# Seven-product input projection: third weight sum in DRAM, one addition in place, new order of products

## The chip, the cores and the metric

The kernel runs on one core of one Trainium2 chip. The metric is the device time of one execution in microseconds (us); a shorter time is better. A profiled execution is recorded by the hardware profiler, and its trace gives the start and end of each instruction on each engine: PE (TensorE, with PEld for its weight loads), DVE (VectorE), ACT (ScalarE), POOL (GpSimd), SP (SyncE, which here only issues transfers). Names with a q behind them (SPq, ACTq, POOLq) are the engines' instruction queues.

## The reference

One decoder layer over 512 tokens of width 2048, in float32. A normed input is projected to 8 heads of forgetting attention ("fox") and 8 heads of a three-branch attention ("nsa"); both are joined, projected back and added to the input; then follows a gated feed-forward network.

```python
def reference(x, attn_norm, w_in, ..., w_gate, w_up, w_down):
    h = _rms_norm(x, attn_norm[l])
    x = x + _hybrid_mixer(h, w_in[l], ...)       # proj = h @ w_in; fox and nsa heads; @ w_out
    h = _rms_norm(x, ffn_norm[l])
    x = x + _swiglu(h, w_gate[l], w_up[l], w_down[l])

# fox head: softmax over past keys of q.k * scale + cum_f[query] - cum_f[key], times v
# with q and k normed per head and cum_f the running sum of log-sigmoid forget gates
```

## The kernel before

Each product is made in full precision from float32 parts: an operand x is split into a high part (ScalarE copies it to the format float32r, line 95) and a low part (VectorE subtracts, line 92), and TensorE sums high times high, high times low and low times high.

The program has four stages. In the first (to about 460 us in the trace) plain projections of 24 tiles of `w_in` run among the heads of nsa. In the second (460 to 730 us) the other 16 tiles, the queries, keys and values of the fox heads 2 to 7, are projected in eight pairs of tiles (`PAIRS`), among the fox heads themselves. The third projects back with `w_out`; the fourth is the feed-forward network (from 908 us). The change concerns the second stage and what prepares it.

A pair isn't projected by eight block products (two halves of the tokens, two tiles, two halves of the depth) but by seven, in the manner of Strassen (`seven`, lines 1049 to 1093). The operands from the activations are `form(f, u)`: f = 0 to 3 lie in `bigm`, f = 4 to 6 are made beforehand by `forms_45` and `forms_6`, and the upper half of `bigm` is made ready for f = 3 by `forms_3`. With the pair's weight blocks b1 = `win[i, 0]`, b2 = `win[i + 1, 0]`, b3 = `win[i, 1]` and b4 = `win[i + 1, 1]` the weight operands are

| product f | weights | from where |
|---|---|---|
| 0 | b1 | loaded |
| 5 | b1 + b2 + b4 | first sum in DRAM (`fsum` 0) |
| 1 | b3 | loaded |
| 4 | b1 + b2 | b2 added in place to the tile of f = 0 |
| 2 | b1 + b2 + b3 + b4 | second sum in DRAM (`fsum` 1) |
| 6 | b4 | loaded |
| 3 | b2 + b4 | b4 loaded, b2 added in place |

That is also their order; in the last pair f = 3 comes before f = 6. A product is 24 matmuls of 128 x 256 (line 1071).

Weights come through three staging tiles of 128 x 1024 float32 (`ws0` to `ws2`, `ws_tile`). `fetch` loads one from SP's queue (line 98) as soon as the parts of its last content are split; `split_w` writes the parts into one of two tiles `wp`, so that ScalarE and VectorE can work one product ahead of TensorE. An addition in place (`add12`, line 1047) is two accumulating transfers of 256 KB on GpSimd's queue, issued after the tile's load has landed and, for f = 4, after the tile has been split for f = 0.

The sums in DRAM are made by transfers from DRAM to DRAM on GpSimd's queue (`sum_weights`, line 141), each of 256 KB, copying or accumulating. `in_weight_sums` makes those of the pairs (20 pieces for two pairs, `GROUP`), `out_weight_sums` those of the projection back (`osum`, 48 pieces). `split_w` issues `paced[0]` of them for each weight split and lets each wait for a split two before it. GpSimd also makes the biases of the scores (`nb`, line 816, and `nbf`, line 845), in the same queue.

Every engine runs its instructions in the order in which the program was put down. `weave`, `gated` and `among` interleave the steps of projections, heads and forms by counts; `stagger` lets the end of a pair (norms of its keys and queries, or transposes of its values) run among the products of the next. `ahead_of` runs generators of forms one behind the other and starts the next one's loads (`xf`, line 968, on ACT's queue) a given number of generators ahead.

## Time and profile before

| | |
|---|---|
| time, median of 3 runs | 2174.6 us (2172.25 to 2176.71) |
| profiled execution | 2173.53 us, of which its span is 2171.5 us |
| mean granted clock of TensorE | 0.982 |
| PE busy | 2092.0 us (96%) |
| DVE busy | 1776.7 us (82%) |
| ACT busy | 1074.8 us (49%) |
| POOL busy | 352.7 us (16%) |
| transfers | 424.78 MB, mean 196 GB/s |

Busy times are sums over the span from the first to the last instruction. In the rows of the trace a transfer or instruction stands as output<-input by the program's names; [4.77 <-ACT wp_kf L95] behind a row says that the engine stood idle 4.77 us before it, until that instruction had ended. A view of waits lists who waited for whom: total us, times, longest.

### The profile page before, as it was taken

The page shows a single profiled execution, that of the slowest core. Times are in us where ns is not written, and L with a number is a line of the kernel's source. Part 1 is how long each engine was busy: PE and PEld are TensorE (multiplying, and loading weights), DVE is VectorE, ACT ScalarE, POOL GpSimd, SP SyncE. Part 2 cuts the span into 40 slices and gives each one's busy share as a digit, 9 for nine tenths or more (in the row PEclk, how much of TensorE's full clock was granted, in tenths as well). Part 3 has the DMA queues.
Part 4 walks back from the last instruction along what each step waited for, and adds up shares of the span by engine and source line. Part 5 has one row for each costly group of instructions (what it writes and reads, how often), then busy time and mean ns, then how long its engine had stood idle before and what let it go on. Part 6 is the DMA issues. An engine that isn't in the chain of part 4 may idle for free.

```text
span 2171.5 us, 40270 instructions
## 1 busy us (share of the span) xinstructions
PE 2092.0 (96%) x16219; PEld 2002.8 (92%) x16219; DVE 1776.7 (82%) x2725; ACT 1074.8 (49%) x1433; POOL 352.7 (16%) x528
## 2 busy tenths in 40 slices
PE   9999999877788899999999999999999999999999
PEld 8888988777787799899999999999999999999999
DVE  6777677655655687899999999999999997879898
ACT  6556465544545555544443434444344455556554
POOL 1133232222332101111111111111111100000000
PEclk9999999988998999999999999999999999999999
DMA  6656455667887557567766777777777798569865
GB/s 217 199 141 133 134 143 140 165 171 183 195 214 165 184 182 239 181 182 193 195 192 179 208 184 202 187 195 191 181 204 185 197 350 291 151 212 328 311 170 153
DMA packets 145644, 424.78 MB, mean 196 GB/s; under 512 B 17768, under 2 KB 17768, under 8 KB 145456
## 3 DMA queue, kind: packets, MB, share of 16 engines
q1 hardware_dynamic: 90016, 285.01, 39.1%
q0 software_dynamic: 43920, 102.00, 25.1%
q10 hardware_dynamic: 11520, 35.18, 4.5%
q8 instruction: 127, 2.08, 0.4%
q14 instruction: 61, 0.50, 0.1%
HBM read 389.86 MB, written 111.95 MB: 231 GB/s over the span
## 4 chain that ended last, share of the span: by engine, by line
PE 79%; DMA 6%; DVE 5%; issue 5%; ACT 4%; POOL 1%; ACTq 0%; SPq 0%; DVEq 0%; POOLq 0%
PE q L1779 39%; PE pd L1918 13%; PE pd L1923 6%; DMA ws_pair<-win 4%; PE po L1363 2%; PE ps_vs L535 2%; DMA xf<-xT 2%; PE ps_kf L1071 1%; PE ps_qn L256 1%; PE ps_qn L257 1%; PE ps_qn L258 1%; PE po L258 1%; PE po L257 1%; PE po L256 1%; ACT wp_kf L95 1%
## 5 line engine op out<-in xcount | busy, mean ns | idle before, releaser
L95 ACT ACTIVATE bigm<-r 128x1792 fp32r<-128x1792 f32 x174 | 298.2, 1714 | 454.2 <-PE q L1779 272.6
L92 DVE TENSOR_TENSOR bigm<-r,bigm 128x1792 fp32r<-128x1792 f32 x174 | 351.4, 2020 | 11.3 <-ACT bigm L95 10.6
L92 DVE TENSOR_TENSOR r<-r 128x512 f32<-128x512 f32 x522 | 267.0, 512 | 27.5 <-DMA r<-wgu 15.1
L141 POOL DMA_DIRECT2D wsum<-wdn x176 | 120.1, 689 | 701.6 <-ACT bigm L95 602.7
L1779 PE MATMUL q<-bigm 128*128 128x256 f32 x1848 | 217.0, 276 | 0.0
L1779 PE MATMUL q<-formy,bigm 128*128 128x256 f32 x1848 | 216.8, 276 | 0.0
L1779 PE MATMUL q<-forma,bigm 128*128 128x256 f32 x1848 | 216.8, 276 | 0.0
L1779 PE MATMUL q<-formx,bigm 128*128 128x256 f32 x1848 | 216.8, 276 | 0.0
L1779 PEld LDWEIGHTS q<-bigm 128*128 128x128 f32 x1848 | 213.1, 188 | 0.0
L1779 PEld LDWEIGHTS q<-forma,bigm 128*128 128x128 f32 x1848 | 213.0, 188 | 0.1
L1779 PEld LDWEIGHTS q<-formy,bigm 128*128 128x128 f32 x1848 | 212.9, 188 | 0.1
L1779 PEld LDWEIGHTS q<-formx,bigm 128*128 128x128 f32 x1848 | 212.9, 188 | 0.0
L1918 PE MATMUL pd<-bigm 128*128 128x256 f32 x1200 | 146.9, 276 | 0.0
L1918 PEld LDWEIGHTS pd<-bigm 128*128 128x128 f32 x1200 | 141.0, 188 | 0.0
L92 DVE TENSOR_TENSOR bigm<-wd,bigm 128x1024 fp32r<-128x1024 f32 (+1 forms) x62 | 107.7, 1738 | 12.5 <-ACT bigm L95 12.4
L95 ACT ACTIVATE bigm<-rawm 128x768 fp32r<-128x768 f32 (+2 forms) x72 | 66.0, 926 | 98.4 <-PE pd L1923 64.1
L1071 PE MATMUL ps_kf<-bigm,wp_kf 128*128 128x256 f32 x576 | 84.2, 305 | 26.7 <-ACT wp_kf L95 26.7
L1071 PEld LDWEIGHTS ps_kf<-bigm,wp_kf 128*128 128x128 f32 x576 | 79.5, 214 | 28.7 <-ACT wp_kf L95 28.7
L92 DVE TENSOR_TENSOR wp_kf<-ws_pair,wp_kf 128x1024 fp32r<-128x1024 f32 x42 | 51.3, 1222 | 55.5 <-ACT wp_kf L95 55.0
L95 ACT ACTIVATE bigm<-wd 128x1024 fp32r<-128x1024 f32 (+1 forms) x62 | 91.1, 1469 | 9.4 <-DVE wd L92 6.1
L92 DVE TENSOR_TENSOR bigm<-rawm,bigm 128x768 fp32r<-128x768 f32 (+2 forms) x72 | 75.5, 1058 | 23.5 <-ACT bigm L95 22.8
L1923 PE MATMUL pd<-bigm 128*128 128x256 f32 x600 | 80.7, 276 | 0.0
(630 smaller groups left out, 4381.1 us busy)
## 6 DMA issues: line engine op xcount, KB each, us to landing
r<-wgu SPq DMA_DIRECT2D x174, 512.0 KB, 4.4
wsum<-wdn POOLq DMA_DIRECT2D x176, 256.0 KB, 5.1
rawm<-ad SPq DMA_DIRECT2D x44, 512.0 KB, 6.7
wd<-wdn SPq DMA_DIRECT2D x40, 512.0 KB, 6.1
wd<-wsum SPq DMA_DIRECT2D x40, 512.0 KB, 7.1
ad<-cb ACTq DMA_DIRECT2D x22, 896.0 KB, 6.5
rawm<-ad SPq DMA_DIRECT2D x44, 384.0 KB, 3.6
ws_pair<-win SPq DMA_DIRECT2D x32, 512.0 KB, 5.0
```

The source lines that it names most:

```text
L92: return pin(nc.vector.tensor_tensor(*args, op=op))
L95: return pin(nc.scalar.activation(*args, **kw))
L141: d = nc.gpsimd.dma_start(step[0], step[1], **step[2])
L256: nc.tensor.matmul(o, lh, rh, start=start, stop=False)
L257: nc.tensor.matmul(o, lh, rl, start=False, stop=False)
L258: nc.tensor.matmul(o, ll, rh, start=False, stop=stop)
L535: nc.tensor.matmul(z[2 * b + t][:, :cols[n]], x[:, xp, at], wp[n][kk], start=(c == 0 and kk == 0 and n == 0 and (t == 0 or gcols is not No ...
L1071: nc.tensor.matmul(z, w[wp][:, u * P:(u + 1) * P], form(f, u)[xp], start=(fresh and m == 0), stop=(m == len(todo) - 1), skip_group_check=True)
L1363: nc.tensor.matmul(q[b][:, h * 256:(h + 1) * 256], w[wp][:, u * P:(u + 1) * P], a[xp], start=(h == 0 and u == 0 and wp == 0 and xp == 0), ...
L1779: nc.tensor.matmul(o, w[wp][:, fb, cs], a[:, xp, fa], start=(k == 0 and h == 0 and wp == 0 and xp == 0), stop=(g == NG - 1 and kk == 1 and ...
L1918: nc.tensor.matmul(b[q][k][:, h * 256:(h + 1) * 256], w[0][:, fb, q * P:(q + 1) * P], a[xp][:, fa], start=(j == 0 and h == 0 and xp == 0), ...
L1923: nc.tensor.matmul(b[q][k][:, h * 256:(h + 1) * 256], w[1][:, fb, q * P:(q + 1) * P], a[0][:, fa], start=False, stop=(j == NJ - 1), skip_g ...
```

## The change

Each pair gets a third sum in DRAM, b2 + b4 (`fsum` 2), which f = 3 loads as it is; the second addition in place is gone. `GROUP` becomes 28. From the second pair on the order is 0, 5, 1, 3, 4, 2, 6: f = 3 goes on in the PSUM bank of f = 5, and three products lie between f = 0 and f = 4 where two did; the first pair keeps 0, 5, 1, 4, 2, 6, 3. `fetch` now takes the next load of one list (`wanted`) into whatever tile has just been split, and first makes sure that the pair's sums have been issued. The number of sums for each split goes from 2, 2.4, 1 and 0.95 to 3, 3, 2 and 0.75 in the four parts of the first two stages. The forms are loaded two generators ahead instead of one, and the first two of `forms_3` start before the stage. In the last pair the saved heads are fetched four steps earlier, and four instead of two heads are split there.

```diff
--- before.py
+++ after.py
@@ -159,9 +159,9 @@
                     yield s[t][:, i], s[t0][:, i], {"accum_op": OP.add}
 
     PAIRS = [("p", h) for h in (2, 3, 4)] + [("v", 4)] + [("p", h) for h in (5, 6, 7)] + [("v", 6)]
-    fsum = {p: [dr.tile([P, 2, T], F32, name=f"fsum{p[0]}{p[1]}{t}") for t in range(2)] for p in PAIRS}
+    fsum = {p: [dr.tile([P, 2, T], F32, name=f"fsum{p[0]}{p[1]}{t}") for t in range(3)] for p in PAIRS}
     FIRST7 = PLAIN
-    GROUP = 20
+    GROUP = 28
     emitted = [0]
 
     def in_weight_sums():
@@ -173,14 +173,14 @@
         for n0 in range(0, len(PAIRS), 2):
             two = [(fsum[PAIRS[n]], blocks(n)) for n in (n0, n0 + 1)]
             cols = [slice(i * T, (i + 1) * T) for i in range(2)]
-            for t, k in ((0, 0), (1, 2)):
+            for t, k in ((0, 0), (1, 2), (2, 3)):
                 for s, b in two:
                     for i in range(2):
                         yield s[t][:, i], b[k][:, cols[i]], {}
-            for k in (1, 3):
+            for t, k in ((0, 1), (2, 1), (0, 3)):
                 for s, b in two:
                     for i in range(2):
-                        yield s[0][:, i], b[k][:, cols[i]], {"accum_op": OP.add}
+                        yield s[t][:, i], b[k][:, cols[i]], {"accum_op": OP.add}
             for s, b in two:
                 for i in range(2):
                     yield s[1][:, i], s[0][:, i], {"accum_op": OP.add}
@@ -931,7 +931,7 @@
         yield
 
     N, NS, F, FS = 18, 25, 53, 13
-    paced[0] = 2
+    paced[0] = 3
     tokens_out = unload()
     weave(ks0, itertools.islice(tokens_out, 2), N, 2, 11)
     weave(stagger(values(("vs0", "vw0"), gcols), normed("kw0", gain(V_WK), "kv"), nsa_q(0), nsa_q(1)),
@@ -1028,23 +1028,35 @@
         return [S[f, u][:, xp] for xp in range(2)]
 
     fetched = {}
-    WS = {0: 0, 5: 1, 1: 2, 2: 1}
-
-    def fetch(n, f):
-        if n == len(PAIRS):
+
+    def products(n):
+        if n == 0:
+            return (0, 0), (1, 5), (0, 1), (2, 4), (1, 2), (2, 6), (0, 3)
+        return (0, 0), (1, 5), (0, 1), (1, 3), (2, 4), (1, 2), (2, 6)
+
+    wanted = iter([(n, f) for n in range(len(PAIRS)) for _, f in products(n) if f != 4])
+
+    def fetch(at):
+        key = next(wanted, None)
+        if key is None:
+            ws_turn.append(at)
             return
+        n, f = key
+        while emitted[0] < GROUP * (n // 2 + 1):
+            sum_weights(highs[-1], osums)
+            emitted[0] += 1
         i = FIRST7 + 2 * n
-        src = {0: win[i, 0], 5: fsum[PAIRS[n]][0], 1: win[i, 1], 2: fsum[PAIRS[n]][1]}.get(f, win[i + 1, 1])
-        if f in (5, 2):
-            src = src.rearrange("p i c -> p (i c)")
-        fetched[n, f] = ws_tile(f"pair{n}_{f}", ws_turn[0] + n + WS.get(f, 2 * ((f == 6) ^ (n == len(PAIRS) - 1))))
-        load(fetched[n, f], src)
-
-    def add12(n, f):
+        src = {0: win[i, 0], 1: win[i, 1], 6: win[i + 1, 1]}.get(f)
+        if src is None:
+            src = fsum[PAIRS[n]][{5: 0, 2: 1, 3: 2}[f]].rearrange("p i c -> p (i c)")
+        fetched[key] = ws_tile(f"pair{n}_{f}", at), at
+        load(fetched[key][0], src)
+
+    def add12(n):
 
         for c in range(2):
             c = slice(c * T, (c + 1) * T)
-            nc.gpsimd.dma_start(fetched[n, f][:, c], win[FIRST7 + 2 * n + 1, 0][:, c], accum_op=OP.add)
+            nc.gpsimd.dma_start(fetched[n, 0][0][:, c], win[FIRST7 + 2 * n + 1, 0][:, c], accum_op=OP.add)
 
     def seven(key, names):
 
@@ -1052,13 +1064,12 @@
         t0, t1 = [ftile(f"t_{name}") for name in names]
         b = []
         lower, upper = slice(0, 256), slice(256, 512)
-        last = [(2, 6), (0, 3)][::-1 if n == len(PAIRS) - 1 else 1]
-        for step, (to, f) in enumerate([(0, 0), (1, 5), (0, 1), (2, 4), (1, 2)] + last):
-            w = split_w(fetched[n, f if f != 4 else 0], HALF * P, f"{names[0]}_{step}", 3)
-            nn, ff = ((n, 0), (n, 2), (n, last[0][1]), (n, last[1][1]), (n + 1, 0), (n + 1, 5), (n + 1, 1))[step]
-            if step:
-                fetch(nn, ff)
-            fresh = f in (0, 5, 4, 3)
+        for step, (to, f) in enumerate(products(n)):
+            st, at = fetched[n, f if f != 4 else 0]
+            w = split_w(st, HALF * P, f"{names[0]}_{step}", 3)
+            if f:
+                fetch(at)
+            fresh = f in (0, 5, 4) or to == 0 and f == 3
             if fresh:
                 b[to:to + 1] = [ps.tile([P, T], F32, tag="ggm"[to], name=f"ps_{names[0]}{to}{step}", bufs=(2, 2, 1)[to])[:, :256]]
             z = b[to]
@@ -1066,8 +1077,8 @@
             for m, (wp, u, xp) in enumerate(todo):
                 if m and m % 6 == 0:
                     yield
-                if m == 12 and step in (0, 3 if last[0][1] == 3 else 4):
-                    add12(n, step and 3)
+                if m == 12 and f == 0:
+                    add12(n)
                 nc.tensor.matmul(z, w[wp][:, u * P:(u + 1) * P], form(f, u)[xp], start=(fresh and m == 0),
                                  stop=(m == len(todo) - 1), skip_group_check=True)
             if f == 0:
@@ -1075,9 +1086,11 @@
             elif f == 5:
                 nc.vector.tensor_tensor(t1[:, lower], z, t0[:, upper], op=OP.add)
             elif f == 4:
-                nc.vector.tensor_tensor(t1[:, upper], z, t1[:, lower], op=OP.subtract)
+                nc.vector.tensor_tensor(t1[:, upper], z, t1[:, upper if n else lower], op=OP.subtract)
             elif f == 1:
                 nc.vector.tensor_tensor(t0[:, lower], z, rstd[:, lower], op=OP.mult)
+            elif f == 3 and to == 1:
+                nc.vector.tensor_tensor(t1[:, upper], z, t0[:, upper], op=OP.add)
             elif f == 6:
                 nc.vector.tensor_tensor(t1[:, lower], z, t1[:, lower], op=OP.subtract)
             elif f == 2:
@@ -1166,24 +1179,25 @@
     less = ap_.tile([P, HALF], F32, name="less")
     nc.vector.tensor_scalar_mul(less, vt[:, V_AN + HALF:V_AN + NK], -1.0)
 
-    paced[0] = 2.4
-    extra = ahead_of([forms_45(u, False) for u in early6], 1)
+    paced[0] = 3
+    extra = ahead_of([forms_45(u, False) for u in early6], 2)
     weave(among(stagger(kf(0), nsa_q(6), nsa_q(7), vf(0), qf(0)), extra, 36, 3), chain(nsa(4), nsa(5), nsa(6), nsa(7)), 6 * NK, 4 * NS, 2)
     run(extra)
     only.close()
     live["x6"] = only.enter_context(tc.tile_pool(name="x6", bufs=1, side="right"))
-    paced[0] = 1
-    extra = ahead_of([forms_45(u, True) for u in range(5, HALF)] + [forms_6(u) for u in early6], 1)
+    paced[0] = 2
+    extra = ahead_of([forms_45(u, True) for u in range(5, HALF)] + [forms_6(u) for u in early6], 2)
     weave(among(stagger(kf(1), qf(1), vf(2)), extra, 2, 2), fox(0), 4 * NK, FS, 18)
     run(extra)
+    extra = ahead_of([forms_3(u) for u in range(HALF)], 2)
+    for _ in range(2):
+        next(extra)
     assert nproj[0] == FIRST7
-    assert emitted[0] >= GROUP * len(PAIRS) // 2, emitted[0]
-    for f in (0, 5, 1):
-        fetch(0, f)
-
-    paced[0] = 0.95
+    for at in [ws_turn.pop(0) for _ in range(3)]:
+        fetch(at)
+
+    paced[0] = 0.75
     side = foxes(range(1, NH - 1))
-    extra = ahead_of([forms_3(u) for u in range(HALF)], 2)
     for n, p in enumerate(PAIRS[:-1]):
         g = stagger((pair if p[0] == "p" else vpair)(p[1]), lag=LAG7)
         gated(among(g, extra, 0, 1) if n == 0 else g, side, 0.5)
@@ -1470,12 +1484,10 @@
             next(side, None)
         elif i % 2 == 0:
             next(last, None)
-        if 16 <= i < 24:
-            fetch_head(order[i - 16])
-        elif i >= 24 and i % 2 == 0:
-            om_parts((i - 24) // 2)
-        if i == 24:
-            ws_turn[0] += len(PAIRS)
+        if 12 <= i < 20:
+            fetch_head(order[i - 12])
+        elif i >= 20 and i % 2 == 0:
+            om_parts((i - 20) // 2)
         if i in (24, 26):
             for _ in range(2):
                 next(pieces[(i - 24) // 2])
@@ -1484,7 +1496,7 @@
     only.close()
 
     def closing():
-        parts = iter(range(2, HALF + LATE[0]))
+        parts = iter(range(4, HALF + LATE[0]))
 
         def part():
             i = next(parts, None)
```

Where the instructions then stand. SP's queue at pair 1 (the names are the staging tile, `ws_pair`, with the number of the pair and f), before:

```order
L98 DMA ws_pair1_0_5206<-win 128x1024
L98 DMA ws_pair1_5_5251<-fsump30_140 128x1024
L98 DMA ws_pair1_1_5289<-win 128x1024
L98 DMA ws_pair1_2_5375<-fsump31_141 128x1024
L98 DMA ws_pair1_6_5407<-win 128x1024
L98 DMA ws_pair1_3_5446<-win 128x1024
L98 DMA ws_pair2_0_5505<-win 128x1024
```

and now:

```order
L98 DMA ws_pair1_0_5251<-win 128x1024
L98 DMA ws_pair1_5_5294<-fsump30_141 128x1024
L98 DMA ws_pair1_1_5332<-win 128x1024
L98 DMA ws_pair1_3_5417<-fsump32_143 128x1024
L98 DMA ws_pair1_2_5449<-fsump31_142 128x1024
L98 DMA ws_pair1_6_5488<-win 128x1024
L98 DMA ws_pair2_0_5546<-win 128x1024
```

The load for f = 3 has moved from the sixth place of the pair to the fourth and comes from a sum (`fsump32`) instead of `win`; those of f = 2 and f = 6 moved back by one.

GpSimd's queue where the sums begin (x2 are the two halves of 256 KB each; `fsump20` is the first sum of pair ("p", 2)), before:

```order
L141 DMA fsump20_138<-win 128x512 x2
L141 DMA fsump30_140<-win 128x512 x2
L141 DMA fsump21_139<-win 128x512 x2
L141 DMA fsump31_141<-win 128x512 x2
L141 DMA fsump20_138<-win 128x512 x2
L141 DMA fsump30_140<-win 128x512 x2
L790 AFFINE_SELECT trif_1164<-trif_1164 128x512
L141 DMA fsump20_138<-win 128x512 x2
L141 DMA fsump30_140<-win 128x512 x2
L141 DMA fsump21_139<-fsump20_138 128x512 x2
L141 DMA fsump31_141<-fsump30_140 128x512 x2
```

and now:

```order
L141 DMA fsump20_138<-win 128x512 x2
L141 DMA fsump30_141<-win 128x512 x2
L141 DMA fsump21_139<-win 128x512 x2
L141 DMA fsump31_142<-win 128x512 x2
L141 DMA fsump22_140<-win 128x512 x2
L141 DMA fsump32_143<-win 128x512 x2
L141 DMA fsump20_138<-win 128x512 x2
L141 DMA fsump30_141<-win 128x512 x2
L141 DMA fsump22_140<-win 128x512 x2
L790 AFFINE_SELECT trif_1175<-trif_1175 128x512
L141 DMA fsump32_143<-win 128x512 x2
L141 DMA fsump20_138<-win 128x512 x2
```

Each pair of pairs gets two more copies and two more additions of two pieces each (`fsump22`, `fsump32`), and the next group follows at once.

ACT's queue where the forms of u = 5 begin (`xf50` and `xf51` are the two raw inputs, loaded by line 968 and first used by line 976), before:

```order
L968 DMA xf50_4371<-xT 128x512
L657 DMA od15_208<-o15_4348 128x512
L968 DMA xf51_4372<-xT 128x512
L95 ACTIVATE fr_qf0_4409<-sq_qf0_4343 64x512
L976 ACTIVATE xf50_4371<-xf50_4371,vt_78 128x512
L968 DMA xf60_4435<-xT 128x512
L431 ACTIVATE qs_qf0_4426<-qs_qf0_4426 128x4
L968 DMA xf61_4436<-xT 128x512
```

and now:

```order
L968 DMA xf50_4411<-xT 128x512
L657 DMA od15_216<-o15_4387 128x512
L968 DMA xf51_4412<-xT 128x512
L968 DMA xf60_4421<-xT 128x512
L968 DMA xf61_4422<-xT 128x512
L976 ACTIVATE xf50_4411<-xf50_4411,vt_78 128x512
L95 ACTIVATE fr_qf0_4451<-sq_qf0_4382 64x512
L968 DMA xf70_4486<-xT 128x512
```

The loads of u = 6 now stand ahead of the first use of those of u = 5, which before stood ahead of them.

More of the change, by code (lines that the diff above doesn't have):

```diff
@@ L218, in parts_tile @@
         return wpl.tile([P, 2 * HALF * P + P], FR, tag="wp", name=name, bufs=2)
-    ws_turn = [0]
+    ws_turn = [0, 1, 2]
     def ws_tile(name, at=None):
         if at is None:
-            at = ws_turn[0] % 3
-            ws_turn[0] += 1
-        return wpl.tile([P, HALF * P], F32, tag=f"ws{at % 3}", name=f"ws_{name}")
+            at = ws_turn.pop(0)
+            ws_turn.append(at)
+        return wpl.tile([P, HALF * P], F32, tag=f"ws{at}", name=f"ws_{name}")
     def raw_w(src, name):
@@ L1030, in hybrid_layer @@
     fetched = {}
[L1031 to L1034 removed]
+    def products(n):
[6 more added lines that the diff above has]
+        if key is None:
+            ws_turn.append(at)
             return
+        n, f = key
+        while emitted[0] < GROUP * (n // 2 + 1):
+            sum_weights(highs[-1], osums)
+            emitted[0] += 1
         i = FIRST7 + 2 * n
[L1037 to L1043 removed]
+        src = {0: win[i, 0], 1: win[i, 1], 6: win[i + 1, 1]}.get(f)
[4 more added lines that the diff above has]
+    def add12(n):
         for c in range(2):
             c = slice(c * T, (c + 1) * T)
[L1047 removed]
+            nc.gpsimd.dma_start(fetched[n, 0][0][:, c], win[FIRST7 + 2 * n + 1, 0][:, c], accum_op=OP.add)
     def seven(key, names):
@@ L1509, in hybrid_layer @@
     run(rest)
-    assert next(osums, None) is None
+    assert next(osums, None) is None, emitted[0]
     paced[0] = 0
```

## The prediction

> **What bounds the kernel now.** I read the stretches of the span first, to see where TensorE is not full, then who waited for whom in the worst of them, then one such wait row by row. The first view gives the busy time of each engine between two moments (start:end, length, then PE, PEld, DVE, ACT, POOL, granted clock, DMA share, GB/s).
>
> ```profile
> 50.00:310.00 260.00, 259.31 (x1494) 224.48 (x1493) 187.74 (x464) 150.50 (x337) 75.23 (x110) 1.00 0.57 151
> 310.00:460.00 150.00, 134.02 (x823) 118.77 (x822) 100.53 (x258) 80.65 (x185) 38.48 (x56) 0.94 0.57 156
> 460.00:730.00 270.00, 215.46 (x1573) 205.87 (x1571) 156.68 (x294) 138.81 (x248) 78.89 (x117) 0.89 0.77 194
> 730.00:908.00 178.00, 176.09 (x1035) 155.32 (x1034) 137.76 (x199) 95.26 (x126) 20.70 (x34) 1.00 0.57 189
> 908.00:2171.50 1263.50, 1258.43 (x11090) 1258.17 (x11089) 1159.67 (x1449) 578.74 (x488) 135.08 (x199) 1.00 0.73 210
> ```
>
> TensorE is full everywhere but in two stretches. From 460 to 730 us, where the eight pairs of heads are projected by seven products each, it idles 270 − 215.5 = 54.5 us, and its granted clock is 0.89, so that of the 215.5 busy us about 215.5 × 0.11 = 24 are slowness. From 310 to 460 us it idles 16 us. What waits in the first of the two:
>
> ```profile
> PE ps_kf L1071 <- ACT wp_kf L95: 26.7, 6, 7.0
> PE s_f L256 <- ACT kf L95: 14.6, 2, 8.4
> PE ps_vf L1071 <- ACT wp_vf L95: 5.7, 1, 5.7
> ...
> ACT wp_kf L95 <- DMA ws_pair<-win: 46.5, 7, 10.2
> ACT wp_vf L95 <- DMA ws_pair<-win: 17.1, 2, 8.9
> ```
>
> TensorE waits 26.7 + 14.6 + 5.7 = 47.0 us for ScalarE, and ScalarE, at its first step on a staged weight tile, waits 63.6 us in nine waits for a transfer into that tile. The first and the last long one, the one in the middle with what surrounds it, and the only short one:
>
> ```profile
> 497.03 2.00 ACT L95 ACTIVATE wp_kf<-ws_pair 128x1024 fp32r<-128x1024 f32 x2 [9.55 <-DMA ws_pair<-win]
> ...
> 638.38 1.07 ACT L95 ACTIVATE wp_kf<-ws_pair 128x1024 fp32r<-128x1024 f32 x1 [0.62 <-DMA ws_pair<-win]
> ...
> 647.76 1.73 POOL L1047 DMA_DIRECT2D ws_pair<-win  x2 [4.43 <-DMA ws_pair<-win]
> 655.70 1.06 ACT L95 ACTIVATE wp_kf<-ws_pair 128x1024 fp32r<-128x1024 f32 x1 [10.22 <-DMA ws_pair<-win]
> 657.33 1.12 PE L256 MATMUL s_f<-kf,qq 128*128 128x512 f32 x2 [8.35 <-ACT kf L95]
> ...
> 719.76 1.06 ACT L95 ACTIVATE wp_vf<-ws_pair 128x1024 fp32r<-128x1024 f32 x1 [8.86 <-DMA ws_pair<-win]
> ```
>
> Counted along the 56 splits, the eight long waits are one in each pair, always the product with f = 3 (the seventh, and the sixth in the last pair). Its tile is loaded, then added to in place (L1047), and only then split. At 647.76 GpSimd had stood 4.43 us for that load; the addition landed at about 655.7; ScalarE stood 10.22 us, and `kf`, queued behind the split, kept TensorE 8.35 us. The other addition in place, that of f = 4, cost one wait of 0.62 us. So **the second addition bounds this stage**, the first one doesn't.
>
> **The change part by part.** Everything is counted from the profiled execution, 2173.5 us (span 2171.5 and 2.0 around it), 1.1 below the median of the three times, 2174.6.
>
> A. The second addition goes. The product f = 3 now takes a sum that lies in DRAM before the stage begins. The 47.0 us above hold one wait that isn't its own, the 4.68 us of the row at 470.62 (below, D). **−42 us**; nothing hides these waits, since TensorE itself stands in them. What is late next is C.
>
> B. After a wait TensorE runs slowly:
>
> ```profile
> 462.95 2.99 PE L1071 MATMUL ps_kf<-f,wp_kf 128*128 128x256 f32 x24 [0.17 <-DVE vf L214]
> 720.87 4.62 PE L1071 MATMUL ps_vf<-bigm,wp_vf 128*128 128x256 f32 x24 [5.72 <-ACT wp_vf L95]
> ```
>
> The same 24 matmuls take 1.6 us longer behind a gap of 5.7 us; elsewhere it is up to 2.7. Eight gaps at about 2 us make **−16 us**, between nothing and the 24 us of the whole stretch.
>
> C. The new wait. From pair 1 on, f = 3 is the fourth product, and its fetch is issued when the tile of the second product is free, two products ahead; all other fetches have three. The rows (ScalarE's split of the second product of pair 1, the fetch that follows it on SP's queue, two later splits) and the landings in this stage (KB each, median us to landing):
>
> ```profile
> 503.54 1.06 ACT L95 ACTIVATE wp_kf<-ws_pair 128x1024 fp32r<-128x1024 f32 x1 [4.51 <-PE ps_kf L1071]
> 505.92 0.33 SPq L98 DMA_DIRECT2D ws_pair<-fsump  x1
> 512.88 1.06 ACT L95 ACTIVATE wp_kf<-ws_pair 128x1024 fp32r<-128x1024 f32 x1 [0.18 <-PE ps_kf L1071]
> 516.17 1.06 ACT L95 ACTIVATE wp_kf<-ws_pair 128x1024 fp32r<-128x1024 f32 x1
> ...
> q0 software_dynamic: 9494, 19.48, 40.9%
> ws_pair<-win SPq DMA_DIRECT2D x30, 512.0 KB, 5.0
> osum<-wos POOLq DMA_DIRECT2D x31, 256.0 KB, 5.2
> ws_pair<-win POOLq DMA_DIRECT2D x30, 256.0 KB, 6.5
> ws_pair<-fsump SPq DMA_DIRECT2D x11, 512.0 KB, 5.2
> osum<-osum POOLq DMA_DIRECT2D x12, 256.0 KB, 5.7
> ```
>
> Split to issue is 505.92 − 503.54 = 2.4 us, landing 5.2, together 7.6. An undisturbed product takes 516.17 − 512.88 = 3.3 to 3.5 us, two of them 6.9. The split of f = 3 then comes 0.7 us late. ScalarE works a product ahead of TensorE, which leaves 3.4 − 1.06 = 2.3 us, so TensorE should not notice before the landing passes 5.2 + 1.6 = 6.8 us. Queued behind that waiting split on ScalarE are the exponentials of the forgetting attention and `kf`, for which the score matmuls wait. The first addition, kept, gets a third product between it and its use (3.4 us more). From pair 1 on, that is; in pair 0 it keeps two, and cost nothing there. The other 54.5 − 42.3 = 12 us of idle time stay, but for D. Against this, work on ScalarE and VectorE that now runs in the shadow of the eight waits comes into the open: they are 139 and 157 us busy, of 220 then. I take **+12 us** (about 1 us of waiting and 0.7 of slowness in each of seven pairs); bounds nothing, and 32 (each fetch as late as the slowest transfer of the stretch, 9.7 us, gives 9.7 − 6.8 = 2.9, and 1.6 of slowness, seven times).
>
> The Trainium skill, "DMA: Bandwidth & Descriptors", section "Anatomy of one DMA — SWDGE (gpsimd) path", fits such a transfer from GpSimd by about 2.0 us and its bytes at 436 GB/s: an estimate of 2.6 us for 256 KB. The row says 6.5. By the page the second addition would land nearly 4 us sooner, A would be −(42 − 8 × 3.9) = −11; the trace has the waits, so A stays.
>
> D. The raw inputs from which the forms of the activations are made come two steps ahead instead of one. Who waits for them between 310 and 480 us, and two rows of the first pair:
>
> ```profile
> DVE acc L978 <- DMA xf<-xT: 10.8, 4, 4.8
> DVE xf L1008 <- DMA xf<-xT: 7.4, 3, 5.1
> DVE xf L1001 <- DMA xf<-xT: 2.7, 2, 2.3
> ACT bigm L200 <- DMA xf<-xT: 6.1, 1, 6.1
> ACT xf L998 <- DMA xf<-xT: 5.0, 3, 3.1
> ...
> 470.62 5.11 PE L1071 MATMUL ps_kf<-bigm,wp_kf 128*128 128x256 f32 x24 [4.68 <-ACT wp_kf L95]
> 478.75 1.97 PE L624 MATMUL pT_f<-ident,p_f 128*128 128x128 f32 x8 [3.02 <-ACT p_f L608]
> ```
>
> VectorE and ScalarE stand 21 and 11 us in front of these loads, with weight splits queued behind. TensorE's share can be no more than its 16 idle us up to 460 and the 7.7 us of the two rows; I take a third, **−8 us**, bounds 0 and −24.
>
> E. Sums earlier. The sums in DRAM grow from 128 to 160 pieces of 256 KB, and some 121 instead of 82 are issued before the stage (23 splits at 3, 12 at 3 and 8 at 2, for 2, 2.4 and 1). GpSimd's groups between 50 and 460 us:
>
> ```profile
> L816 POOL TENSOR_SCALAR nb<-E,qs_qn 128x512 f32<-128x512 f32 (+1 forms) x64 | 41.3, 656 | 54.1 <-DVE st_s L595 19.1 <-DVE st_w L595 9.1 <-DVE qs_qn L437 5.3
> L141 POOL DMA_DIRECT2D fsump<-win x45 | 31.5, 767 | 128.4 <-ACT wp_kw L95 39.4 <-ACT wp_qn L95 27.6 <-ACT wp_vs L95 16.5
> ```
>
> 39 × 0.77 = 30 us of issue on a GpSimd busy 75 of 260 us, and, at the stage's 0.409 × 270 / 73 = 1.5 us of all DMA engines for each (30 + 31 + 12 software transfers), 59 us of transfer over 410 us: a share of 0.57 becomes 0.71, less than the 0.77 of the later stage. Hidden behind TensorE, unless the distance biases `nb` come late behind a sum that waits: **+3 us**, bounds 0 and 15. In the stage itself software transfers fall from 78 to 55, about −35 us of 208, so the share stays near 0.78 in a stage of 220 us, and landings as they are.
>
> F. Seven fewer VectorE evictions, heads fetched four steps and two more splits done earlier at the end: 0, as 176.1 of the next 178 us are busy already; 2 us either way.
>
> Sum: 2173.5 − 42 − 16 + 12 − 8 + 3 = **2122.5 us**.
>
> **The rivals.**
>
> *The fetch of f = 3 becomes the new wait.* For it: it has two products where the others have three, and 0.7 us are missing at the median. Against it: 2.3 us of reserve and a DMA share that stays. Price: C at its bound of 32 instead of 12, **2142 us**. The Trainium skill, same page, section "Latency and other measured facts", gives 0.2 us on average and 2 us at high load for an access to HBM; no row here splits a landing so, but such a load would use up the reserve. Chance 0.15.
>
> *ScalarE and VectorE bound the stage.* The forgetting heads' chain (scores, minimum, exponential, transposes) has a fixed place between products. Were half of the idle time won lost to it, A is 21 and B 8: 2122.5 + 29 = **2151 us**. For it: VectorE would be busy 157 of 220 us. Against it: it is busy 137.8 of 178 us after 730 with TensorE full. Chance 0.10.
>
> *The earlier sums cost more than the stage gains, slower.* Place: GpSimd's queue between 50 and 310 us, where a sum that adds one sum to another waits for a landing (5 to 6 us) with `nb` behind it; VectorE needs `nb`, and TensorE has no idle time there to lose. From a mean delay of 51 / 64 = 0.8 us for each of the 64 `nb` on, it decides; at 1.1 us it gives **2193 us**. Against it: `nb` idles 54.1 us now, waiting for VectorE, and TensorE does not see it. Chance 0.04.
>
> *The change doesn't do what it says*: the wait belongs to any load at this place, and f = 3 from DRAM waits as long: A and B nil, C nil, **2169 us**. Against it: the five loads of each pair that are split as they land have no long wait. The 5 us count as no change. Chance 0.03.
>
> **How the numbers follow.** The forecast has the rest, 0.68, and by itself reaches from 2100 to 2140. With the first two rivals and the joint ends of B, C and D cut to what is likely, 2096 to 2150 leaves out about 2 in 10. About 0.2% (4 us) is what a measurement of this kernel can tell from no change: faster 0.92, same 0.03, slower 0.05.
>
> **What would show it.** A and B: no wait of ScalarE for `ws_pair` over 3 us, the stage near 220 us, its clock 0.95 or more. C: waits of the fourth split in each pair, for a load from `fsum`, about 1 us or less. D: waits for `xf` under 10 us in all. E: TensorE still over 258 of 260 us before 310. The prediction is wrong if ScalarE's waits move to another product with their length, or if idle time appears before 310 us.

## The result, and the profile after

The changed kernel takes **2119.2 us** (median of four runs, 2115.8 to 2119.8), the kernel before 2173.4 us on the same chip. The ratio is 0.9749, with a 95% interval from 0.9728 to 0.977. The forecast was 2122.5. The profiled execution of the changed kernel took 2119.1 us, its span is 2117.3 us. One execution of e11 below, the profiled one, was 33 us slower than its other four and is left out, so that e11 has no row for the stage.

First the busy time of each engine by stretches, in the same columns as before the change. The third stretch is cut at the first and the last matmul of the seven products, the fourth ends at the first matmul of the feed-forward projection.

```profile
50.00:310.00 260.00, 257.00 (x1477) 222.19 (x1476) 185.62 (x454) 147.74 (x331) 91.55 (x135) 1.00 0.70 179
310.00:460.00 150.00, 137.09 (x861) 119.71 (x860) 103.14 (x267) 83.52 (x189) 46.83 (x68) 0.98 0.67 175
454.40:674.00 219.60, 201.69 (x1571) 192.90 (x1570) 156.82 (x292) 140.97 (x254) 69.86 (x95) 0.97 0.79 213
674.00:853.00 179.00, 176.02 (x1039) 154.32 (x1038) 138.00 (x200) 94.52 (x124) 20.55 (x35) 1.00 0.57 192
```

The same two cuts in the kernel before:

```profile
459.60:728.50 268.90, 214.35 (x1568) 205.09 (x1567) 155.18 (x292) 137.50 (x246) 78.89 (x117) 0.89 0.77 192
728.50:907.60 179.10, 177.19 (x1040) 156.10 (x1038) 138.86 (x202) 96.76 (x128) 20.70 (x34) 1.00 0.57 191
```

The stage of the seven products is 268.9 − 219.6 = 49.3 us shorter and begins 459.6 − 454.4 = 5.2 us earlier. Together that is the 2173.53 − 2119.06 = 54.5 us that the two profiled executions differ by; what follows lasts 179.0 where it lasted 179.1. In the stage TensorE's idle time falls from 54.6 to 17.9 us, and its busy time, for the same matmuls, from 214.4 to 201.7 at a clock of 0.97 instead of 0.89. Before 310 us its idle time rises from 0.7 to 3.0.

Who waits in the stage now, TensorE first (total, times, longest):

```profile
PE ps_kf L1082 <- ACT wp_kf L95: 9.2, 6, 5.9
PE pT_f L624 <- ACT p_f L608: 3.1, 3, 1.2
PE vT L1146 <- DVE pt_f L92: 2.2, 1, 2.2
...
ACT wp_kf L95 <- DMA ws_pair<-fsump: 10.5, 5, 2.8
```

The 47 us for which TensorE stood behind ScalarE are 9.2, and ScalarE's 63.6 us in front of `ws_pair<-win` are gone from the list; in their place it waits for `fsump`. Row by row, the two largest gaps of TensorE, both in pair 0, and then the first three waits of ScalarE for a third sum:

```profile
463.78 5.49 PE L1082 MATMUL ps_kf<-f,wp_kf 128*128 128x256 f32 x24 [5.88 <-ACT wp_kf L95]
471.60 4.41 PE L1082 MATMUL ps_kf<-bigm,wp_kf 128*128 128x256 f32 x24 [2.34 <-ACT wp_kf L95]
...
498.56 1.06 ACT L95 ACTIVATE wp_kf<-ws_pair 128x1024 fp32r<-128x1024 f32 x1 [2.61 <-DMA ws_pair<-fsump]
524.99 1.06 ACT L95 ACTIVATE wp_kf<-ws_pair 128x1024 fp32r<-128x1024 f32 x1 [1.43 <-DMA ws_pair<-fsump]
552.13 1.06 ACT L95 ACTIVATE wp_vf<-ws_pair 128x1024 fp32r<-128x1024 f32 x1 [1.48 <-DMA ws_pair<-fsumv]
```

So f = 3 still waits in each of pairs 1 to 7, 12.3 us in all (10.5 for `fsump`, 1.8 for `fsumv`), but on ScalarE. Six of these waits pass by TensorE with gaps under 0.75 us, one reaches it, by way of VectorE (ScalarE's split, VectorE's half of the split, the transposed probabilities behind it, TensorE):

```profile
579.24 1.06 ACT L95 ACTIVATE wp_kf<-ws_pair 128x1024 fp32r<-128x1024 f32 x1 [2.21 <-DMA ws_pair<-fsump]
580.33 1.23 DVE L92 TENSOR_TENSOR wp_kf<-ws_pair,wp_kf 128x1024 fp32r<-128x1024 f32 x1 [3.52 <-ACT wp_kf L95]
581.47 1.28 DVE L92 TENSOR_TENSOR pt_f<-pT_f,pt_f 128x512 fp32r<-128x512 f32 x2
582.21 1.11 PE L1146 MATMUL vT<-ident,t_vf 128*128 128x128 f32 x4 [2.18 <-DVE pt_f L92]
```

TensorE loses most in pair 0, 8.2 of its 17.9 idle us. There ScalarE makes the forms of f = 3 from raw inputs ahead of the weight split, and waits for VectorE's part of them:

```profile
459.23 0.51 ACT L200 ACTIVATE bigm<-xf,vt 128x256 fp32r<-128x256 f32 x1 [3.15 <-DVE xf L1008]
461.94 0.51 ACT L200 ACTIVATE bigm<-xf,vt 128x256 fp32r<-128x256 f32 x1 [2.21 <-DVE xf L1008]
462.67 1.06 ACT L95 ACTIVATE wp_kf<-ws_pair 128x1024 fp32r<-128x1024 f32 x1
```

### The profile page after: what moved, and what is told of

It is laid out like the page before. It is cut to its first block, busy times and chain, and to the rows that moved or that the text cites. A ratio compares the mean times of both kernels' runs of the same rounds, so it can differ in the third digit from the quotient of the medians.

```text
span 2117.3 us, 40258 instructions
## 1 busy us (share of the span) xinstructions
PE 2076.1 (98%) x16219; PEld 1985.4 (94%) x16219; DVE 1776.4 (84%) x2718; ACT 1075.5 (51%) x1433; POOL 368.4 (17%) x544
## 4 chain that ended last, share of the span: by engine, by line
PE 84%; DVE 5%; ACT 4%; DMA 3%; issue 2%; POOL 1%; ACTq 0%; SPq 0%; DVEq 0%; POOLq 0%
PE q L1791 40%; PE pd L1930 13%; PE pd L1935 6%; PE ps_kf L1082 2%; PE po L1377 2%; PE ps_vs L535 2%; PE ps_vf L535 1%; PE po L258 1%; PE ps_qn L256 1%; PE po L256 1%; DMA ws_pair<-fsump 1%; PE po L257 1%; PE ps_qn L258 1%; PE ps_qn L257 1%; DMA xf<-xT 1%
## 5 line engine op out<-in xcount | busy, mean ns | idle before, releaser
L92 DVE TENSOR_TENSOR bigm<-r,bigm 128x1792 fp32r<-128x1792 f32 x174 | 351.5, 2020 | 10.7 <-ACT bigm L95 10.2
L1082 PE MATMUL ps_kf<-bigm,wp_kf 128*128 128x256 f32 x576 | 79.2, 288 | 3.2 <-ACT wp_kf L95 3.2
L141 POOL DMA_DIRECT2D fsump<-win x72 | 53.6, 840 | 152.7 <-ACT wp_ks L95 37.4
L1082 PEld LDWEIGHTS ps_kf<-bigm,wp_kf 128*128 128x128 f32 x576 | 73.9, 194 | 5.2 <-ACT wp_kf L95 4.6
```

The lines of the kernel that those rows point to most:

```text
L92: return pin(nc.vector.tensor_tensor(*args, op=op))
L141: d = nc.gpsimd.dma_start(step[0], step[1], **step[2])
L1082: nc.tensor.matmul(z, w[wp][:, u * P:(u + 1) * P], form(f, u)[xp], start=(fresh and m == 0), stop=(m == len(todo) - 1), skip_group_check=True)
```

## The experiments

Each was measured beside the kernel before on the same chip, in four to six executions; e5 to e8 ran on another chip than the other experiments, and the median of the kernel before differs by up to 1.7 us between the sessions. "Start" and "length" are those of the stage (first to last matmul of the seven products) in each run's profiled execution. This is one execution, from 5.3 us below its kernel's median (e1) to 4.9 above (e4; e10 and e12 are 4.1 and 4.4 above), so lengths that differ by a few us tell little. In e4, e5 and e7 f = 3 is also the last product of pair 7, where it reads forms that the next stage has already overwritten; their output for that pair is another, the work is the same.

| kernel | median us | ratio, 95% interval | start | length |
|---|---|---|---|---|
| before | 2173.4 to 2175.1 | 1 | 459.6 | 268.9 |
| changed | 2119.2 | 0.9749 (0.9728–0.9770) | 454.4 | 219.6 |
| e1 third sum and pace, alone | 2119.6 | 0.9748 (0.9729–0.9768) | 461.5 | 208.8 |
| e2 pace alone | 2160.2 | 0.9936 (0.9921–0.9951) | 463.2 | 251.0 |
| e3 inputs alone | 2162.3 | 0.9947 (0.9929–0.9965) | 446.8 | 266.7 |
| e4 changed, f = 3 added in place, lead 3 | 2162.5 | 0.9951 (0.9934–0.9967) | 453.8 | 268.7 |
| e5 changed, f = 3 last everywhere | 2114.0 | 0.9719 (0.9703–0.9734) | 455.5 | 215.3 |
| e6 changed, f = 3 lead 1 | 2135.0 | 0.9820 (0.9804–0.9837) | 452.0 | 234.4 |
| e7 changed, f = 3 added in place, lead 4 | 2137.4 | 0.9836 (0.9817–0.9855) | 453.1 | 238.3 |
| e8 changed, forms later in pair 0 | 2116.8 | 0.9730 (0.9711–0.9750) | 456.1 | 214.0 |
| e9 f = 3 last, forms later | 2108.6 | 0.9707 (0.9692–0.9722) | 453.1 | 210.4 |
| e10 third sum alone, 73 sums in the stage | 2135.5 | 0.9828 (0.9813–0.9842) | 461.8 | 232.3 |
| e11 f = 3 last in pairs 0 to 6 | 2113.5 | 0.9723 (0.9705–0.9742) | – | – |
| e12 third sum alone, old pace | 2133.0 | 0.9806 (0.9791–0.9821) | 461.7 | 216.6 |

### Is it the second addition? e1, e4, e5

e1 puts only the third sum (with its tile, its load and 28 pieces a group) and the changed pace into the kernel before:

```diff
-            for t, k in ((0, 0), (1, 2)):
+            for t, k in ((0, 0), (1, 2), (2, 3)):
...
-            for k in (1, 3):
+            for t, k in ((0, 1), (2, 1), (0, 3)):
...
-                if m == 12 and step in (0, 3 if last[0][1] == 3 else 4):
+                if m == 12 and step == 0:
...
-    paced[0] = 2
+    paced[0] = 3
...
-    paced[0] = 2.4
+    paced[0] = 3
...
-    paced[0] = 1
+    paced[0] = 2
...
-    paced[0] = 0.95
+    paced[0] = 0.75
```

> The kernel before with the third sum in DRAM (f = 3 is loaded complete, no second addition in place, 28 sums a group at the changed kernel's pace), and nothing else: before's order of the products, three products between each fetch and its use, raw inputs one ahead. Theory: the second addition in place is what the stage waited for, so A and B come whole with E's price: 2173.4 - 42 - 16 + 3, about 2118, and with the work that comes into the open 2115 to 2125; no wait of ScalarE for a weight tile over 3 us from pair 1 on. Rival (the gain is the new order and the earlier inputs): 2150 or more. Rival (any load at this place waits): 2169 or more.

It took 2119.6 us, the whole gain of the change. Its stage:

```profile
461.50:670.30 208.80, 197.25 (x1568) 189.65 (x1567) 155.68 (x292) 137.18 (x246) 68.94 (x95) 0.98 0.82 221
```

And all that ScalarE still waits there for a weight tile (both times the tile of the first addition, in pairs 5 and 3):

```profile
ACT wp_kf L95 <- DMA ws_pair<-win: 1.5, 1, 1.5
ACT wp_vf L95 <- DMA ws_pair<-win: 0.5, 1, 0.5
```

TensorE idles 11.6 us instead of 54.6 and is busy 17.1 us less. The new order and the earlier inputs are not in this kernel, so they are not what gains. The pace is in it; what it is worth by itself is asked of e2, e10 and e12 below.

e4 goes the other way. It takes the changed kernel and makes f = 3 by a load and an addition in place again, as the last product of each pair:

```diff
-        src = {0: win[i, 0], 1: win[i, 1], 6: win[i + 1, 1]}.get(f)
+        src = {0: win[i, 0], 1: win[i, 1], 6: win[i + 1, 1], 3: win[i + 1, 1]}.get(f)
...
-        return (0, 0), (1, 5), (0, 1), (1, 3), (2, 4), (1, 2), (2, 6)
+        return (0, 0), (1, 5), (0, 1), (2, 4), (1, 2), (2, 6), (0, 3)
...
+                if m == 12 and step == 4:
+                    add12(n, 3)
```

> The changed kernel with f = 3 made by the second addition in place again, three products after its fetch and as the last product of each pair, as in the kernel before; sums, pace, inputs and the rest as changed (the third sums are still made, and read by nobody). Theory: the eight long waits of ScalarE are back, 6 to 10 us each, and TensorE loses 42 us and 16 of slow clock: 2165 to 2177. Rival (the earlier sums and inputs carry the gain): 2120 to 2140.

2162.5 us, a little under the expected 2165, and ScalarE's waits are back as they were, 43.9 + 17.1 = 61.0 us:

```profile
ACT wp_kf L95 <- DMA ws_pair<-win: 43.9, 8, 8.8
ACT wp_vf L95 <- DMA ws_pair<-win: 17.1, 2, 8.6
```

e5 has the same order of products as e4 (the second piece of its diff) and keeps the third sum.

> The changed kernel with the order of its pair 0 in every pair: f = 3 is the last product and has three products between fetch and use, the addition to f = 0 keeps two before its use. Theory: ScalarE's 12.3 us of waits for the sums of f = 3 go, but TensorE did not see them, so the time stays: 2115 to 2121, and no new wait over 1 us for the tile of f = 4. Rival (C was worth its 12 us): 2105 to 2110. Rival (the addition to f = 0 comes late with two products): 2125 or more.

It took 2114.0 us, so the second addition costs 2162.5 − 2114.0 = 48.5 us, its own transfers included (e4 has 67 transfers from GpSimd's queue in the stage, e5 51); by the ratios, since the two ran on different chips, it is 50. e5 is also 5.3 us faster than the changed kernel, 1 us below what my theory allowed, so the waits for the third sum seem not to be wholly hidden. (The two intervals overlap a little, 0.9703 to 0.9734 and 0.9728 to 0.9770.) The second half of the expectation failed: the tile of f = 4 is now waited for, 1.7 us in pair 3 and 1.6 in pair 5.

### Is it the addition, or the length of its chain? e7

e7 is e4 with f = 3 fetched one product earlier, in exchange with f = 6, and the addition issued one product earlier:

```diff
-    wanted = iter([(n, f) for n in range(len(PAIRS)) for _, f in products(n) if f != 4])
+    wanted = iter([(n, f) for n in range(len(PAIRS)) for f in (0, 5, 1, 2, 3, 6)])
...
-                if m == 12 and step == 4:
+                if m == 12 and step == 3:
```

> The changed kernel with f = 3 made by the second addition in place again, but fetched four products before its use instead of three (f = 6 gets two instead of three), the addition issued a product earlier as well. Theory (the length of the chain load, addition, split decides): each of the eight waits is one product, 3.4 us, shorter, so TensorE loses some 2 us and 1 of slow clock a pair: 2142 (2130 to 2155). Rival (a second addition costs its whole price wherever it stands, by GpSimd or the transfers): 2165 or more. Rival (one more product was all that lacked): 2117 to 2125.

It took 2137.4 us, 25.1 under e4, as the theory had it. The stage is 268.7 − 238.3 = 30.4 us shorter than e4's, and ScalarE's waits for `win` are halved to 30.5 us:

```profile
ACT wp_kf L95 <- DMA ws_pair<-win: 25.3, 12, 5.8
ACT wp_vf L95 <- DMA ws_pair<-win: 5.2, 2, 4.6
```

They are shorter by as much again, 30.5 / 8 = 3.8 us a pair, for one product of 3.4 us more. So half of the addition's price does not follow it wherever it stands: the chain of load, addition and split was too long for the products between. The other half stays (e7 is 23.4 us above e5). How much of it is the rest of the chain and how much the 16 transfers more was not separated.

### The lead of f = 3: e6, e11

e6 takes the lead of f = 3 from two products to one, from pair 1 on, by the order of the fetches:

```diff
-    wanted = iter([(n, f) for n in range(len(PAIRS)) for _, f in products(n) if f != 4])
+    wanted = iter([(n, f) for n in range(len(PAIRS)) for f in ((0, 5, 1, 2, 3, 6) if n else (0, 5, 1, 2, 6, 3))])
```

> The changed kernel with the fetches of f = 3 and f = 2 exchanged from pair 1 on: f = 3 has one product between fetch and use instead of two, f = 2 has four. Theory: the split of f = 3 comes 3.4 us later, some 5.2 us late in all, of which a reserve of 2.3 us on TensorE takes part: 2.9 us and about 1 us of slow clock in seven pairs, 28 us, 2147 (2135 to 2155). Rival (TensorE's reserve is deeper, since the score matmuls of the forgetting heads fill the gap): 2119 to 2127.

It costs 15.7 us, not 28; the 2135.0 us lie at the lower edge of the theory's range. In pair 2, the splits of the third and the fourth product on ScalarE and the gap that TensorE then has:

```profile
522.90 1.07 ACT L95 ACTIVATE wp_kf<-ws_pair 128x1024 fp32r<-128x1024 f32 x1
530.54 1.04 ACT L95 ACTIVATE wp_kf<-ws_pair 128x1024 fp32r<-128x1024 f32 x1
531.63 4.61 PE L1082 MATMUL ps_kf<-bigm,wp_kf 128*128 128x256 f32 x24 [1.83 <-ACT wp_kf L95]
```

The split comes 7.6 us behind the last one, 4.2 later than a product of 3.4 us would have it, and TensorE loses 1.8. In pair 4:

```profile
587.11 1.06 ACT L95 ACTIVATE wp_kf<-ws_pair 128x1024 fp32r<-128x1024 f32 x1 [1.72 <-DMA ws_pair<-fsump]
588.22 1.65 PE L1082 MATMUL ps_kf<-bigm,wp_kf 128*128 128x256 f32 x12 [1.40 <-ACT wp_kf L95]
```

Over pairs 1 to 7 the split comes 6.8 to 8.4 us behind the last one, 7.6 on average, and TensorE loses 0.2 to 3.5 us at it, 12.5 in all; a reserve of 2.3 us behind 4.2 of lateness would give 13. So the reserve held on average, and the lateness was smaller than the 5.2 us that I had put in. But the run is not as clean as its edit. Unlike what "The kernel before" says of the order of instructions, the kernel doesn't hold them to the order of the program in this stage (`pinned`, which does that, is set only behind it), and ScalarE's queue came out differently: in pair 2 the norms of the pair before (L318, L319) now stand ahead of this split, where in the changed kernel they stand behind it, and ScalarE doesn't wait for the load at all. In e1, e10 and e12, which are compared below, ScalarE and TensorE have the same order.

e11 gives f = 3 its third product back in pairs 0 to 6, and leaves pair 7:

```diff
-        if n == 0:
+        if n < len(PAIRS) - 1:
             return (0, 0), (1, 5), (0, 1), (2, 4), (1, 2), (2, 6), (0, 3)
```

> The changed kernel with f = 3 as the last product in pairs 0 to 6, in the last pair still the fourth, and nothing else. Theory: the 5 us that the same order in all eight pairs gained come from the waits of pairs 1 to 6, so they come here too: 2113 to 2117. Rival (they come from the last pair alone): 2118 to 2121.

2113.5 us (the middle of four executions, from 2108.0 to 2116.8), 5.7 under the changed kernel. The two intervals overlap again, so no single run shows it; together e5 and e11 make it likely that the moved-up f = 3 costs about 5 us. Against the profile of e5, TensorE in the changed kernel idles 1.9 us more in the stage and is busy 2.4 us longer. The row at 582.21 above shows 2.2 us; the rest can't be assigned to single rows.

### What do the sums' transfers cost? e2, e10, e12

e2 changes the pace only (the last piece of e1's diff).

> The kernel before with only the pace of the sums changed (3, 3, 2, 0.75 where it was 2, 2.4, 1, 0.95): the same 128 sums, more of them before the stage. Theory: hidden behind TensorE but for a few late distance biases, +3 (2173 to 2179), with POOL busier and TensorE's idle time before 310 us up from 0.7 to some 3 us. Rival (fewer sums inside the stage also free its transfers, so that the additions land sooner): 2165 or less.

The rival was right: 13.9 us faster, with the second addition still there. The stage in that kernel:

```profile
463.20:714.20 251.00, 210.58 (x1568) 200.64 (x1567) 155.32 (x291) 137.15 (x246) 55.28 (x79) 0.92 0.64 167
```

ScalarE's waits in it:

```profile
ACT wp_kf L95 <- DMA ws_pair<-win: 37.0, 7, 8.2
ACT wp_vf L95 <- DMA ws_pair<-win: 10.6, 2, 9.0
```

And its landings (queue with packets, MB and share of the DMA engines; then count, KB each, median us). Software transfers are those from GpSimd's queue, here the additions and the sums:

```profile
q0 software_dynamic: 5344, 9.72, 24.9%
ws_pair<-win SPq DMA_DIRECT2D x30, 512.0 KB, 3.5
ws_pair<-fsump SPq DMA_DIRECT2D x11, 512.0 KB, 5.6
ws_pair<-win POOLq DMA_DIRECT2D x30, 256.0 KB, 5.3
```

Only five sums are left in the stage; software transfers there fall from 73 to 35, their queue's share from 41% to 25%. The load from `win` lands in 3.5 us instead of 5.0, the addition in 5.3 instead of 6.5 (the load from a sum takes 5.6 instead of 5.2), and ScalarE's waits fall from 63.6 to 47.6 us.

Does this gain stand beside that of the third sum? e10 has the third sum at before's pace ahead of the stage, so that more sums fall into it:

```diff
-    paced[0] = 0.95
+    paced[0] = 1.45
```

> The kernel before with the third sum in DRAM and before's pace ahead of the stage (2, 2.4, 1); inside the stage 1.45 sums a split, so that all 160 are still made: some 78 of them stand in the stage instead of 53 at before's pace or 37 at the changed one. Theory: with the second addition gone no wait is left that a quicker landing would shorten, so the earlier sums gain nothing here and their cost of 3.6 us ahead of the stage is saved: 2113 to 2120. Rival (the 14 us that the pace alone gained are part of the 54): 2128 to 2136.

2135.5 us: again the rival, and my theory, that nothing waits for transfers any more, was wrong. By the trace 73 sums stand in the stage and 15 transfers of the first addition, 88 in all. The stage:

```profile
461.80:694.10 232.30, 206.70 (x1565) 197.47 (x1566) 156.04 (x291) 136.63 (x245) 91.53 (x132) 0.94 0.91 240
```

And its landings:

```profile
q0 software_dynamic: 10756, 23.48, 52.0%
ws_pair<-win SPq DMA_DIRECT2D x22, 512.0 KB, 6.3
ws_pair<-win POOLq DMA_DIRECT2D x15, 256.0 KB, 7.1
```

e12 has before's pace throughout and makes the last 25 sums behind the stage:

```diff
         for g in (late[0], side, last):
             for _ in g:
                 part()
+                [sum_weights(highs[-1], osums) for _ in range(2)]
                 yield
...
```

> The kernel before with the third sum in DRAM and before's own pace ahead of the stage and in it (2, 2.4, 1, 0.95): the same number of sums stands in the stage as before, 16 additions in place fewer, and the last 25 sums are made behind the stage, two a step. With 78 sums in the stage the time was 2135.5, with 37 of them 2119.6. Theory (the stage pays for its software transfers only near saturation, its DMA share was 0.91 with 78 sums and 0.82 with 37): with 53 the share is below what it was and the waits do not come back: 2115 to 2122, so the second addition alone is worth 52 to 58. Rival (each transfer in the stage costs its part in proportion, 16 us for 41 sums): 2124 to 2128, so the second addition alone is worth 46 to 50.

The number of sums in the stage was not held: the kernel before runs out of sums and has 43 there, e12 has 55. All software transfers, with the additions, are nearly equal, 73 and 69. The total, 2133.0, is above both expectations, since the 25 sums are not free behind the stage either. The stage, and what follows it:

```profile
461.70:678.30 216.60, 201.05 (x1567) 192.81 (x1566) 155.89 (x292) 137.18 (x245) 80.72 (x113) 0.96 0.85 229
678.30:720.00 41.70, 29.74 (x139) 24.16 (x139) 20.88 (x40) 18.66 (x36) 15.73 (x24) 0.84 0.98 249
```

The largest gap of TensorE there:

```profile
709.29 1.97 PE L624 MATMUL pT_f<-ident,p_f 128*128 128x128 f32 x8 [8.36 <-ACT p_f L608]
```

They crowd into 42 us with the DMA engines 0.98 busy, and TensorE idles 12.0 us there; from the stage's end to the feed-forward projection it takes 193.8 us instead of e1's 178.3. The stage itself gives part of the answer. With the third sum it lasts 208.8, 216.6 and 232.3 us with 51, 69 and 88 software transfers in it (e1, e12, e10). The totals of e10 and e1, which start the stage at the same time, differ by 15.9 us in the median, so that 37 transfers cost 0.43 us each on average, with no second addition that waits for them; in e2 it was 17.9 / 38 = 0.47, with it. Whether the price is even or begins only at a higher load, as my theory for e12 had it, stays open: of the 7.8 us between e1 and e12, 6.6 lie in pairs 0 and 3 alone, and their two profiles lie 5.3 us below and 4.4 above their medians, which is more than the difference.

### The inputs and pair 0: e3, e8, e9

e3 gives the kernel before only the earlier raw inputs:

```diff
-    extra = ahead_of([forms_45(u, False) for u in early6], 1)
+    extra = ahead_of([forms_45(u, False) for u in early6], 2)
...
+    extra = ahead_of([forms_3(u) for u in range(HALF)], 2)
+    for _ in range(2):
+        next(extra)
     assert nproj[0] == FIRST7
```

> The kernel before with only the raw inputs of the forms two steps ahead instead of one, and the first two of the f = 3 forms started before the stage. Theory: 8 us of TensorE's idle and slow time before and at the start of the stage go, 2165 (2160 to 2170). Rival (these waits are hidden, and what is gained before the stage is waited off in it, since the additions in place set its end): 2172 to 2175.

11.8 us faster; the stage starts at 446.8 instead of 459.6 and is 2.2 us shorter, so what is gained ahead of the stage isn't waited off in it. In the changed kernel, which has the earlier sums as well, the start is 454.4, so 7.6 of the 12.8 us are lost again (e4 to e9, which all have both, start between 452.0 and 456.1). The earlier sums alone, in e2, made the start 3.6 us later; the rest was not separated.

e8 moves the forms of f = 3 back within pair 0:

```diff
-        gated(among(g, extra, 0, 1) if n == 0 else g, side, 0.5)
+        gated(among(g, extra, 4, 2) if n == 0 else g, side, 0.5)
```

> The changed kernel with the f = 3 forms of the activations made from the fifth step of pair 0 on, in every second step, instead of from its first step on in every step; their first two raw inputs are still fetched before the stage. Theory: ScalarE's split of the second product no longer stands behind a form that waits for its raw input, so TensorE's 5.9 and 2.3 us at 464 and 472 us go with 2 us of slow clock: 2109 to 2114. Rival (the forms then stand in the way of later products, or the stall is the exponentials' own): 2117 to 2123.

2116.8 us, between theory and rival, with an interval that holds no change too. The gap of 5.9 us is gone, but others take part of its place:

```profile
PE pT_f L624 <- ACT p_f L608: 5.0, 4, 1.9
PE ps_kf L1082 <- ACT bigm L200: 2.2, 1, 2.2
PE ps_kf L1082 <- ACT wp_kf L95: 1.8, 4, 0.8
```

e9 is e11 and e8 together.

> The changed kernel with f = 3 as the last product in pairs 0 to 6 (in the last pair it stays the fourth) and with the f = 3 forms made later in pair 0 (from the fifth step on, every second step). Theory: the seven waits for the sums of f = 3 and the stall of pair 0 are different places, so their gains of 5.2 and 2.5 us add: 2109 to 2113. Rival (what either gains is waited off at the forgetting heads' chain of exponentials, which sets the end of the stage near 670 us in the runs so far): 2113 to 2117.

2108.6 us, 0.4 below the expected range and the fastest kernel here: 10.7 us under the changed one, which was measured at another time (9 by the ratios). Its interval, 0.9692 to 0.9722, lies below the changed kernel's. Its stage lasts 210.4 us, close to e1's 208.8, and starts 8.4 us earlier.

## Why the prediction held, step by step

The total was 3.3 us off, and that is in part luck: the sum is better than its terms. From the kernel before through e12 and e1 to the changed one, the profiled executions split their 54.5 us so: the start of the stage +1.9 (459.6 to 461.5; e12, with before's pace, starts at 461.7), the second addition −52.3 (268.9 to 216.6), the sums moved out of the stage −7.8 (to 208.8), the inputs −7.1 (start 461.5 to 454.4), and +10.8 for what the new order and pair 0 give back (208.8 to 219.6; 2.7 of it in pair 0, 4.5 in pair 4, where the gap of 2.2 us is). So A and B were some 6 us too large and E some 9 too dear, and these errors cancel. The split is good to some 5 us a term only: by the medians e1 and the changed kernel differ by 0.4 us, which would make the +10.8 about 6.7.

- **A and B**, −42 and −16. The mechanism was right. At nearly the same number of software transfers (e12) TensorE's idle time falls by 39.0 and its busy time by 13.3 us; in e1, with fewer, by 43.0 and 17.1. e4 and e5 give 48.5 for both together. The 2.7 us of slowness that B names beside its rows is more than they show: the most that 24 matmuls in one piece take behind a gap in that kernel's stage is 5.11 us, 2.1 over the 2.99. The estimate from the Trainium skill ("DMA: Bandwidth & Descriptors", section "Anatomy of one DMA — SWDGE (gpsimd) path"), 2.6 us for such an addition and −11 for A, does not hold here: with the lightest load, in e2, the addition still landed in 5.3 us.
- **C**, +12. The mechanism was right, the size was not. The fourth split waits for `fsum` 12.3 us, more than the 1 us or less a pair that I expected to see, but the order that causes it costs about 5 us (e5, e11). I had counted a loss on TensorE in all seven pairs, while the reserve of 2.3 us of the same paragraph covers most of the waits of 0.3 to 2.8; e6 agrees with this reserve on the average of its pairs, with the reservation made there. Where a wait came through, it came by VectorE's queue, which I had not followed. The work of ScalarE and VectorE that was to come into the open adds nothing that shows: e1 has next to no wait for weights left to hide it behind, and the shortest stage.
- **D**, −8. The start is 7.1 us earlier than e1's, but pair 0 takes part of it. TensorE's 4.68 and 3.02 us there, which I had counted among the gains, became 5.88 and 2.34. Waits for the raw inputs between 310 and 480 us fall from 39.7 to 17.0, not below 10. (The five rows of the prediction add up to 32.0 of the 39.7; two more of ScalarE were left out, so that it stood there 18.8 us and not 11.) The largest row now:

```profile
DVE acc L978 <- DMA xf<-xT: 8.7, 1, 8.7
```

- **E**, +3, is **the step that failed**. Ahead of the stage it went nearly as put down: TensorE is busy 257.0 of 260 us before 310, where the sign asked for over 258, and e1 starts as e12 does (461.5 and 461.7). The stage starts 3.6 us later in e2, though, and beside the earlier inputs 7.6 later than with the inputs alone (e3). What was wrong is that the transfers taken out of the stage were given no value, from a DMA share that stays and "landings as they are". With the second addition in place the new pace shortens the stage by 17.9 us and the whole by 13.9 (e2), where E had +3. With the third sum, 37 transfers are worth 15.9 us (e10 and e1); at an even price the 18 between e12 and e1 are worth 7.7, and their profiles give 7.8. The median landings did stay: in the changed kernel a load from `win` takes 4.6 us (5.0 before), one from a sum 5.3 (5.2), an addition 6.6 (6.5). So landings that stay don't mean that the transfers cost nothing. By which of them the stage gains was not found.
- **F**, 0. The stretch behind the stage lasts 179.0 us as before. From pair 5 to the end of the stage the changed kernel, e5, e8 and e9 need 75.5 to 76.2 us, e1 73.4, and e12, without the new head fetches, 75.0; whether the fetches, the order in the last pair or the spread between executions make the difference was not separated.

The rivals: the fetch of f = 3 did become a new wait, but mostly ScalarE's, and cost about 5 us where the rival had 32. ScalarE and VectorE don't bound the stage: in e1 VectorE is busy 155.7 of 208.8 us and TensorE loses 11.6. The slower rival, late distance biases before 310 us, did not come, at 0.70 DMA share and 91.6 us of GpSimd. That any load at this place waits is excluded by e1.

## What to carry to other kernels

Follow one tile from its fetch to its use and add up the chain against the work between; a chain of two transfers can need one step more than a chain of one, and moving its fetch by a step is the cheapest test (e7, 25 us, with f = 3 still added in place). When background transfers are moved, price the place they leave as well as the place they go to: here 37 of them cost 15.9 us in the busy stage, though the median landings of the changed kernel hardly differ from those before. Parts that gain by themselves need not add up (inputs alone 11.8 us, pace alone 13.9, pace and third sum 54.5, the whole change 54.2), so they should be measured apart and together.
